# The first seven-product tile's weight forms of the second feed-forward, ordered behind the turned rows of the last block

## The chip, the cores and the metric

The kernel is one program on one core of a Trainium2 chip. It computes a whole decoder layer for 512 tokens. The metric is the device time of one execution in microseconds (us); several runs are taken and the median stands. The engines are TensorE (PE; its weight loads are listed as PEld), VectorE (DVE), ScalarE (ACT), GpSimd (POOL) and SyncE (SP, which here only issues transfers). Each engine works through its own queue of instructions in the order in which they stand in the program, and waits for the others by semaphores.

## The reference

The layer has a first feed-forward, a mixer (dilated attention and a recurrence, gated and merged), and a second feed-forward. Every part has a root-mean-square norm ahead of it and one behind it. The change is at the seam between the mixer's output product and the second feed-forward:

```python
def rms_norm(x, g):
    y = x * lax.rsqrt(jnp.mean(x * x, axis=-1, keepdims=True) + NORM_EPS)
    return y * g

def swiglu(x, w_gate, w_up, w_down):
    return (jax.nn.silu(x @ w_gate) * (x @ w_up)) @ w_down

    ...
    h = h + rms_norm(merged @ w_out[l], mix_norm_post[l])

    f = swiglu(rms_norm(h, ffn2_norm_pre[l]), ffn2_w_gate[l], ffn2_w_up[l], ffn2_w_down[l])
    h = h + 0.5 * rms_norm(f, ffn2_norm_post[l])
```

There are 512 tokens, the model is 1024 wide and the feed-forward 2816, which is 22 tiles of 128 columns. Everything is float32.

## The kernel before

**Products in three.** Each float32 operand is split into a high part (ACT, a copy to a shorter format, line 269) and a low part (DVE, the difference, line 270). A product is three matmuls: high by high, high by low, low by high.

**The seam.** The output product of the mixer works on token rows, in four blocks of 128 tokens. When a block's sums are done, `Boundary.block` works out its scale from the sum of squares (lines 342 to 344 and 383), adds the block to the residual h (DVE, line 475), stores h by a POOL transfer (line 476), squares the new h with a running sum (ACT, line 478), takes the second scale (ACT line 390, DVE lines 342 to 344) and writes the normed rows u in two halves (DVE, line 483). `Boundary.turn` then turns these rows into columns: TensorE transposes (line 491) into a bank, ACT and DVE write the high part (line 494) and the low part (line 495), and ACT copies the bank to `facc` as well (line 496).

**The second feed-forward.** Its first three tiles of 128 columns (0 to 2) are ordinary products of gate and up weights. `gemm_first` runs the first five of the six weights in two halves of 256 tokens (lines 284 to 286): the first half of the tokens, which needs blocks 0 and 1 only, for all five weights, and then the second half. The turns of blocks 2 and 3 are called behind the third and the fourth weight of the first half. So the last block's rows have to be turned before the second half begins. The sixth weight follows in `ffn`.

**Seven-product tiles.** The other 19 tiles (3 to 21) are done by a scheme that needs seven products of half size in place of eight, with forms that are sums of quarters. The forms of x are made in three steps (lines 610 to 616 and splits). For each tile `w_forms_in_place` reads one raw block of up and gate weights of 1 MB and makes four splits (7 forms) from it, with four sums in place (lines 652 to 658). `prod` (from line 1008 on) runs the products in the order p1, p5, p6, p2, p7, p3, p4. In the first such tile ACT copies the bank behind p1 (line 1016), and p6 adds onto the same bank. DVE adds the pieces of the result (line 1021): one of these sums reads the bank behind p7, and p4 adds onto that bank.

**Buffers.** Raw weights have two buffers of 1 MB; SP issues a load (line 215) as soon as a buffer's readers are through. Split weights have four wide slots (`w8`) and two narrow ones (`w4`). The four wide ones are held by the first four ordinary weights while the seam is worked on. Of a seven-product tile's four splits, one is narrow (`d`).

**What sets the order.** The code is traced in program order, and a planner then writes each engine's queue: of the instructions that are ready by its own estimate of the times, the one with the best priority goes next. `high_priority` moves a block of code ahead in priority (the weight forms by 100 steps, the emptying of banks by 200). `tc.issue_after(ins)` adds an order edge: what is traced in its block on the engine of `ins` is put behind `ins` in that engine's queue, without a wait for its end. In `ffn`, `behind(*engines)` uses this with the dictionary `last`, which holds the last instruction of each engine that was named: the forms of a tile are made in `behind("DVE", "ACT")`, so behind the last DVE and ACT instruction of the product before. The dictionary starts empty, so the forms of the first two seven-product tiles, 3 and 4, which are made before any product has run, have no edge.

Of the kernel before, what the change touches and what calls it, by code (L numbers as in the profile page):

```python
# [10 lines left out]
F32 = mybir.dt.float32  # L11
F32R = mybir.dt.float32r
AF = mybir.ActivationFunctionType
# [141 lines left out]
def hybrid_layer(ctx: ExitStack, tc: tile.TileContext, xT: bass.AP, xN: bass.AP, wst: bass.AP,  # L155
                 first: bass.AP, rows: bass.AP, wdn: bass.AP, wbig: bass.AP, consts: bass.AP, bias: bass.AP, out: bass.AP):
    nc = tc.nc
    DVE, ACT, PE = nc.vector, nc.scalar, nc.tensor
# [19 lines left out]
    def new_h():  # L178
        hs["t"] = [bpool.tile([P, 4, T], F32, name="h", tag="b") for _ in range(2)]
# [9 lines left out]
    def fb(b, sl=slice(0, D)):  # L189
        return facc[:, 2 * b:2 * b + 2, :].rearrange("p k t -> p (k t)")[:, sl]  # L190
# [51 lines left out]
    def big(shape, dt=F32R):  # L242
        return bpool.tile(shape, dt, name="big", tag="b")
# [24 lines left out]
    def split(dh, dl, src):  # L268
        ACT.activation(dh, src, AF.Copy)  # L269
        DVE.tensor_sub(dl, src, dh.bitcast(F32))  # L270

    def acc_ps():
        turns["acc"] += 1
        return banks[(turns["acc"] - 1) % turns["n"]]

    def aux_ps():
        turns["aux"] += 1
        return banks[turns["of"][(turns["aux"] - 1) % len(turns["of"])]]
# [26 lines left out]
    def gemm_first(keys, x, slots, then):  # L305


        wts = [fetch(k, None if i < 4 else slots.pop(0)) for i, k in enumerate(keys)]
        pss = [acc_ps() for _ in keys]
        for sl in HALVES:  # L310
            for i, (wt, ps) in enumerate(zip(wts, pss)):
                for k in range(x.n):
                    mm3(ps[:, sl], k128(wt[0])[:, k, :], k128(wt[1])[:, k, :], x.hi[k][:, sl],
                        x.lo[k][:, sl], k == 0, k == x.n - 1)
                if sl.start == 0:
                    for f in then.get(i + 1, ()):
                        f()
        return pss
# [91 lines left out]
    FHALVES = (slice(0, T), slice(T, D))  # L410
# [54 lines left out]
    class Boundary:  # L465
# [21 lines left out]
        def turn(self, b):  # L487
            for i, u in enumerate(self.u.pop(b)):
                ps = aux_ps()
                for j in range(4):  # L490
                    PE.transpose(ps[:, j * P:(j + 1) * P], u[:, j * P:(j + 1) * P], ident)
                src = ps.rearrange("p (k t) -> p k t", k=4)
                hi, lo = (t[:, :, b * P:(b + 1) * P] for t in (self.his[i], self.los[i]))
                ACT.activation(hi, src, AF.Copy)
                DVE.tensor_sub(lo, src, hi.bitcast(F32))
                ACT.activation(fb(b, FHALVES[i]), ps, AF.Copy)

    def act_of(his, los):
        return Act([his[k // 4][:, k % 4, :] for k in range(8)], [los[k // 4][:, k % 4, :] for k in range(8)])
# [54 lines left out]
    def tx_slot(pool, bufs=1):  # L554
        return pool.tile([P, 2, 4, HB], F32R, name="tx", tag="tx", bufs=bufs)

    def forms_of(x, his, los, pool, copied, places={}):


        spool[0] = pool  # L560
        fx = facc.rearrange("p k t -> p (k t)").rearrange("p (b c) -> p b c", b=4)

        def quarter(i, j):
            return fx[:, 2 * j:2 * j + 2, i * T:i * T + T]

        def slot():
            return tx_slot(pool, 1 if copied else 2).rearrange("p s k t -> p s (k t)").rearrange(
                "p s (b c) -> p s b c", b=2)

        x01, x10, x11 = quarter(0, 1), quarter(1, 0), quarter(1, 1)  # L570
        t, d = {}, {}
        for name, i, j in (("p1", 0, 0), ("p2", 1, 0), ("p3", 1, 1)):
            t[name] = tuple(z[i][:, :, HALVES[j]] for z in (his, los))

        def copies():
            for name in ("p1", "p2", "p3"):
                v = big([P, 2, 4, HB])
                for i in range(2):
                    nc.gpsimd.dma_start(v[:, i], t[name][i])
                t[name] = v[:, 0], v[:, 1]  # L580

        def form(name, v, src):
            t[name] = tuple(v[:, i].rearrange("p b (k t) -> p k b t", k=4) for i in range(2))
            split(v[:, 0], v[:, 1], src)

        def first():
            d[1], d[2] = (pool.tile([P, 2, T], F32, name="ts", tag="s", bufs=2) for _ in range(2))
            DVE.tensor_sub(d[1], quarter(0, 0), x01)
            DVE.scalar_tensor_tensor(d[2], x11, -1.0, d[1], op0=ALU.mult, op1=ALU.subtract)
            form("p6", slot(), d[2])  # L590

        def second():
            DVE.tensor_sub(x01, x11, x01)
            form("p7", places["p7"](), x01)

        def third():
            DVE.scalar_tensor_tensor(d[2], d[2], -1.0, x10, op0=ALU.mult, op1=ALU.subtract)
            form("p4", slot(), d[2])

        def fourth():  # L600
            form("p5", places["p5"](), d[1])

        if not copied:
            return t, [first, second, third, fourth]

        def early():
            if copied:
                copies()
            d[1], d[2] = (pool.tile([P, 2, T], F32, name="ts", tag="s", bufs=2) for _ in range(2))
            DVE.tensor_sub(d[1], quarter(0, 0), x01)  # L610
            DVE.scalar_tensor_tensor(d[2], x11, -1.0, d[1], op0=ALU.mult, op1=ALU.subtract)
            DVE.tensor_sub(x01, x11, x01)

        def middle():
            form("p6", slot(), d[2])
            DVE.scalar_tensor_tensor(d[2], d[2], -1.0, x10, op0=ALU.mult, op1=ALU.subtract)
            form("p5", big([P, 2, 2, T]), d[1])

        def late():
            form("p7", big([P, 2, 2, T]), x01)  # L620
            form("p4", big([P, 2, 2, T]) if copied else slot(), d[2])

        return t, [early, middle, late]
# [189 lines left out]
        def rows(self):  # L813
            return self.ub.rearrange("p (s k) t -> p s (k t)", s=2)

    def ffn(n, x, r, forms_x, home, pss):
        t, steps = forms_x
        n0 = NSTD[n]
        ub, wdt, dr = home.ub, home.wd, home.dr
# [50 lines left out]
        def last_act(f):  # L870
            v = home.slot((f - LAST[0] - 1) % 8)
            return v[:, 0, :], v[:, 1, :]
# [108 lines left out]
                    else:  # L981
                        add(u0, True)

        last = {}

        @contextmanager
        def behind(*engines):
# [141 lines left out]
        last = Act(*zip(*(last_act(f) for f in range(*LAST))))  # L1129
# [16 lines left out]
    pss = [acc_ps() for _ in range(4)]  # L1146
# [12 lines left out]


    end1 = ffn(1, u1, r1, x_forms("g1a", r1, ap1), home1, pss)
    new_h()
    for b in range(4):
# [19 lines left out]
    with ExitStack() as mx:  # L1183
# [17 lines left out]
        pss = [acc_ps() for _ in range(4)]  # L1201
# [226 lines left out]
    with ExitStack() as mx:  # L1428
# [130 lines left out]
        for hd in range(NH):  # L1559
# [9 lines left out]
            for kind, c in FILL[hd]:  # L1569
                if kind == "attn":  # L1570
                    ws = fetch((kind, c))
                    for i in range(2):
                        ps = acc_ps()
                        gemm(ps, [w[:, i * T:(i + 1) * T] for w in ws], attn)
                        DVE.tensor_mul(facc[:, 2 * c + i, :], ps, facc[:, 2 * c + i, :])
                else:
                    ps = acc_ps()
# [10 lines left out]
        for c in range(KC):  # L1588
            ps = acc_ps()
# [6 lines left out]
    ap2 = ctx.enter_context(tc.tile_pool(name="act2", bufs=1))  # L1596
    home2 = Home(ap2)
    his, los = ([home2.act[:, 8 * i + 4 * s:8 * i + 4 * s + 4, :] for i in range(2)] for s in range(2))
    u2 = act_of(his, los)
    kept = dpool.tile([4, P, D], F32, name="kept")  # L1600
    grow3, grow4 = gains(home2.rows(), 2, 3)
    bd2 = Boundary(1.0, grow4, his, los, kept)
# [3 lines left out]
    keys = [(w, 2, i) for i in range(NSTD[2]) for w in ("gate", "up")]  # L1606
    pss = gemm_first(keys[:NFIRST], u2, [home2.spare()[2]],
                     {3: [lambda: bd2.turn(2)], 4: [lambda: bd2.turn(3)]})
    end2 = ffn(2, u2, None, forms_of(u2, his, los, ap2, True), home2, pss)
    new_h()  # L1610
    for b in range(4):
        nc.gpsimd.dma_start(hb(b), kept[b])
# [132 lines left out]
```

## Time and profile before

| what | value |
|---|---|
| median of 3 runs | 1223.34 us (1223.24 to 1223.8) |
| the profiled execution's own time | 1223.28 us |
| its span, first to last instruction | 1221.2 us |
| mean granted TensorE clock | 0.999 |
| the seam: first transposes of the last block | 888.66 us into the span |
| first seven-product tile of the second feed-forward: first product | 911.70 us |

A row of the timeline reads: start, duration, engine, line, operation, what is written `<-` what is read, shapes, and in brackets how long the engine stood idle before it and what ended that. When a row has x2 or more, instructions that follow each other are merged. A row of the waits reads: who waited, for whom, total us, number of times, longest. A row of the chain that ended last reads: start, duration, what. A row of stretches reads: the stretch, its length, then busy us and count of TensorE, its weight loads, DVE, ACT and POOL, then the granted clock, the DMA share and GB/s. ACT and DVE instructions overlap a little at their ends, so starts are the better measure of a sequence.

### The profile page before, as it was taken

Reading aid. Unit: us, or ns where it says so; the run is one execution under the profiler, and the core shown is the slowest. Engines: PE = TensorE matmul, PEld = TensorE weight load, DVE = VectorE, ACT = ScalarE, POOL = GpSimd, SP = SyncE. Lnnn points to the kernel's source line nnn. Section 1 sums busy time; section 2 is a strip of 40 time slices with the busy share of each in tenths; the row PEclk is TensorE's granted clock in tenths of the full one; section 3 lists DMA queues with packets and bytes.
Section 4 is the critical chain, followed back from the end, with each engine's and each line's share of the span. In section 5 each row is a group of like instructions: output and inputs, shape, how many; then the busy total and the mean of one; then the engine's idle time right before and its main releaser. Section 6 shows DMA issues by size and latency. Waiting matters only on the chain.

```text
span 1221.2 us, 19573 instructions
## 1 busy us (share of the span) xinstructions
PE 1209.9 (99%) x7790; PEld 1102.6 (90%) x7790; DVE 984.0 (81%) x1540; ACT 746.0 (61%) x1238; POOL 84.5 (7%) x139
## 2 busy tenths in 40 slices
PE   9999999999999999999999999999999999999998
PEld 8898989999878899999999888888899999999996
DVE  7998878988579888888776998755789887979864
ACT  6566665655656564666666788634566665656452
POOL 0001111100102000000001000000110110101000
PEclk9999999999999999999999999999999999999999
DMA  6336646464735222223235223524462655555441
GB/s 247 138 104 173 170 111 171 141 163 121 255 116 176 105 82 101 78 79 104 70 138 202 75 91 141 183 101 164 132 190 87 182 155 146 159 136 163 114 156 69
DMA packets 37452, 167.63 MB, mean 137 GB/s; under 512 B 4209, under 2 KB 7665, under 8 KB 25329
## 3 DMA queue, kind: packets, MB, share of 16 engines
q1 hardware_dynamic: 18432, 107.13, 25.2%
q0 software_dynamic: 18928, 59.25, 18.1%
q8 instruction: 61, 1.00, 0.3%
q14 instruction: 31, 0.25, 0.1%
HBM read 153.79 MB, written 8.39 MB: 133 GB/s over the span
## 4 chain that ended last, share of the span: by engine, by line
PE 93%; DVE 4%; issue 1%; DMA 1%; ACT 1%; DVEq 0%; ACTq 0%
PE bank L1008 10%; PE bank L1009 9%; PE bank L1010 9%; PE bank L284 7%; PE bank L286 7%; PE bank L285 7%; PE bank L675 6%; PE bank L676 6%; PE bank L677 6%; PE bank L923 4%; PE bank L922 4%; PE bank L924 4%; PE bank L405 3%; PE bank L406 3%; PE bank L404 3%; DVE w L270 1%
## 5 line engine op out<-in xcount | busy, mean ns | idle before, releaser
L270 DVE TENSOR_TENSOR w<-raw,w 128x1024 fp32r<-128x1024 f32 (+1 forms) x276 | 300.6, 1100 | 61.9 <-ACT w L269 56.0
L269 ACT ACTIVATE w<-raw 128x1024 fp32r<-128x1024 f32 (+1 forms) x276 | 258.9, 956 | 102.4 <-PE bank L286 40.1
L1008 PE MATMUL bank<-big,w 128*128 128x256 f32 x840 | 240.6, 286 | 2.5 <-ACT c L1016 0.9
L1009 PE MATMUL bank<-big,w 128*128 128x256 f32 x840 | 237.5, 283 | 0.0
L1010 PE MATMUL bank<-big,w 128*128 128x256 f32 x840 | 236.2, 283 | 0.0
L1008 PEld LDWEIGHTS bank<-big,w 128*128 128x128 f32 x840 | 160.8, 191 | 7.3 <-ACT c L1016 1.9
L1009 PEld LDWEIGHTS bank<-big,w 128*128 128x128 f32 x840 | 160.9, 192 | 1.6
L1010 PEld LDWEIGHTS bank<-big,w 128*128 128x128 f32 x840 | 160.3, 192 | 0.0
L922 PE MATMUL bank<-wd,act 128*128 128x512 f32 x224 | 87.8, 392 | 0.0
L923 PE MATMUL bank<-wd,act 128*128 128x512 f32 x224 | 87.8, 392 | 0.0
L924 PE MATMUL bank<-wd,act 128*128 128x512 f32 x224 | 87.2, 389 | 0.0
L675 PE MATMUL bank<-big,w 128*128 128x256 f32 x252 | 73.0, 290 | 0.0
L677 PE MATMUL bank<-big,w 128*128 128x256 f32 x252 | 71.5, 284 | 0.0
L676 PE MATMUL bank<-big,w 128*128 128x256 f32 x252 | 71.2, 283 | 0.0
L1016 ACT ACTIVATE c<-bank 128x256 f32<-128x256 f32 x72 | 27.5, 382 | 61.3 <-PE bank L1010 60.8
L270 DVE TENSOR_TENSOR wd<-npair,wd 128x1024 fp32r<-128x1024 f32 x24 | 29.4, 1224 | 37.7 <-ACT wd L269 37.7
L284 PE MATMUL bank<-act,w 128*128 128x512 f32 (+1 forms) x168 | 58.6, 354 | 0.0
L285 PE MATMUL bank<-act,w 128*128 128x512 f32 (+1 forms) x168 | 58.5, 349 | 0.0
L286 PE MATMUL bank<-act,w 128*128 128x512 f32 (+1 forms) x168 | 58.5, 349 | 0.0
L284 PE MATMUL bank<-big,w 128*128 128x512 f32 x144 | 56.0, 389 | 0.0
L285 PE MATMUL bank<-big,w 128*128 128x512 f32 x144 | 56.0, 389 | 0.0
L286 PE MATMUL bank<-big,w 128*128 128x512 f32 x144 | 56.0, 389 | 0.0
(399 smaller groups left out, 3208.7 us busy)
## 6 DMA issues: line engine op xcount, KB each, us to landing
raw<-in_w SPq DMA_DIRECT2D x90, 1024.0 KB, 4.9
dr<-in_wdn POOLq DMA_DIRECT2D x40, 512.0 KB, 5.8
npair<-in_wdn POOLq DMA_DIRECT2D x32, 512.0 KB, 5.5
big<-act POOLq DMA_DIRECT2D x6, 512.0 KB, 4.1
h<-in_x SPq DMA_DIRECT2D x8, 256.0 KB, 5.2
h<-in_xn POOLq DMA_DIRECT2D x4, 512.0 KB, 5.2
raw<-in_wbig SPq DMA_DIRECT2D x2, 1024.0 KB, 4.8
kept_m<-h POOLq DMA_DIRECT2D x4, 512.0 KB, 2.9
```

Source lines behind the costliest of these rows:

```text
L269: ACT.activation(dh, src, AF.Copy)
L270: DVE.tensor_sub(dl, src, dh.bitcast(F32))
L284: PE.matmul(ps, wh, xh, start=first, stop=False)
L285: PE.matmul(ps, wh, xl, start=False, stop=False)
L286: PE.matmul(ps, wl, xh, start=False, stop=last)
L675: PE.matmul(ps, wh, xh, start=start and k == 0, stop=False, skip_group_check=True)
L676: PE.matmul(ps, wh, xl, start=False, stop=False, skip_group_check=True)
L677: PE.matmul(ps, wl, xh, start=False, stop=k == 3, skip_group_check=True)
L922: PE.matmul(ps, xh, wh, start=start and k == 0, stop=False, skip_group_check=True)
L1008: PE.matmul(ps, wh, xh, start=start and k == 0, stop=False, skip_group_check=True)
L1009: PE.matmul(ps, wh, xl, start=False, stop=False, skip_group_check=True)
L1010: i = PE.matmul(ps, wl, xh, start=False, stop=k == 3, skip_group_check=True)
```

## The change

The turn keeps the last DVE and the last ACT instruction that it wrote, and the second feed-forward's dictionary `last` starts with these two in place of empty. The first feed-forward still starts with an empty one. So the weight forms of tile 3, and those of tile 4, stand behind the last turned rows of the last block in the queues of DVE and ACT.

```diff
@@ Boundary.turn
                 ACT.activation(hi, src, AF.Copy)
-                DVE.tensor_sub(lo, src, hi.bitcast(F32))
-                ACT.activation(fb(b, FHALVES[i]), ps, AF.Copy)
+                i_dve = DVE.tensor_sub(lo, src, hi.bitcast(F32))
+                i_act = ACT.activation(fb(b, FHALVES[i]), ps, AF.Copy)
+            self.last = {"DVE": i_dve.ins, "ACT": i_act.ins}
@@ ffn
-    def ffn(n, x, r, forms_x, home, pss):
+    def ffn(n, x, r, forms_x, home, pss, after={}):
...
-        last = {}
+        last = dict(after)
@@ the call
-    end2 = ffn(2, u2, None, forms_of(u2, his, los, ap2, True), home2, pss)
+    end2 = ffn(2, u2, None, forms_of(u2, his, los, ap2, True), home2, pss, bd2.last)
```

The dictionary is used where the forms are made:

```python
            elif ev[0] == "prep":
                with behind("DVE", "ACT"):
                    forms[ev[1]] = w_forms_in_place(("gu", n, ev[1]))
```

## The prediction

> **What bounds the kernel now.** I read the page's busy times first, then the waits of TensorE, then the chain that ended last around the place of the change, then the three queues' timelines there.
>
> ```profile
> span 1221.2 us, 19573 instructions
> PE 1209.9 (99%) x7790; PEld 1102.6 (90%) x7790; DVE 984.0 (81%) x1540; ACT 746.0 (61%) x1238; POOL 84.5 (7%) x139
> ...
> PE bank L491 <- DVE u L483: 1.4, 1, 1.4
> ```
>
> TensorE is busy for 1209.9 of 1221.2 us, so the kernel is bound by TensorE, and a change that adds or removes no matmul can win only what TensorE idles. The longest single wait is that of the transposes of the last boundary block (L491) for the DVE instruction that makes their rows (L483). It stands at this place of the TensorE queue:
>
> ```profile
> 886.97 0.28 PE L286 MATMUL bank<-act,tx 128*128 128x256 f32 x1
> 888.66 0.63 PE L491 MATMUL bank<-cst,u 128*128 128x128 f32 x4 [1.42 <-DVE u L483]
> ```
>
> The gap is 1.42 us: 886.97 + 0.28 = 887.25 to 888.66. The chain that ended last says what made the rows late:
>
> ```profile
> 876.95 6.54 DMA raw<-in_w
> 883.52 0.64 ACT w L269
> 884.18 0.70 DVE w L270
> 884.91 0.70 DVE raw L654
> 885.63 0.69 DVE raw L655
> 886.40 0.60 DVE act L495
> 887.07 0.60 DVE act L495
> 887.77 0.76 DVE u L483
> ```
>
> The raw weights of seven-product tile 3 land at 883.49; one split of them (ACT L269, DVE L270) and two sums (L654, L655) follow, and only behind these the work on the last block. That this work had been ready earlier is seen on ACT and DVE:
>
> ```profile
> 880.86 1.28 DVE L475 SCALAR_TENSOR_TENSOR h<-facc,stat,h 128x1024 f32<-128x1024 f32 x1
> ...
> 883.52 0.63 ACT L269 ACTIVATE w<-raw 128x512 fp32r<-128x512 f32 x1 [4.18 <-DMA raw<-in_w]
> 884.05 1.04 ACT L478 ACTIVATE facc<-h 128x1024 f32<-128x1024 f32 x1
> ...
> 885.57 0.28 ACT L390 ACTIVATE stat<-stat,eps 128x1 f32<-128x1 f32 x1
> ...
> 884.18 0.69 DVE L270 TENSOR_TENSOR w<-raw,w 128x512 fp32r<-128x512 f32 x1 [2.04 <-ACT w L269]
> ...
> 886.25 0.15 DVE L342 SCALAR_TENSOR_TENSOR stat<-stat 128x1 f32<-128x1 f32 x1
> ```
>
> The square of the last block (L478) had its rows at 880.86 + 1.28 = 882.14, but ACT stood 4.18 us in front of the weight split, waiting for the load, and the square came at 884.05, 1.91 us later. DVE stood 2.04 us in the same way.
>
> **The change, part by part.** The two names kept in turn and the copied dictionary issue nothing. They add order edges from the last DVE and ACT instruction of the last block's turn to every DVE and ACT instruction of the weight forms of tiles 3 and 4; an edge within one queue is no wait and costs nothing by itself. Of these forms all but four instructions already stand behind the turn (the first other one, tile 3's next split, is on ACT at 898.73), so what moves is one ACT instruction of 0.63 us (883.52) and three DVE instructions (884.18, 884.91, 885.63; from 884.18 to the next one at 886.25 they take 2.07 us). No DMA moves: the raw load is outside the edges, on SP, and waits only for its buffer. POOL gets nothing new; its copies of the turned forms wait for the turn and can only come sooner.
>
> Step 1, the stall. With the split gone from ahead of it, L478 starts at 882.14. From its start to the end of L390 it took 884.05 to 885.85, so 1.80; L390 ends at 883.97. From the first DVE step (886.25) to the end of the first half of the rows (887.77 + 0.76 = 888.53) it took 2.28, with two turned forms of the block before it in between, to which nothing is added: the first half is there at about 886.3, the second some 0.7 later, and TensorE asks at 887.25. The stall goes with 0.3 to 1 us to spare: -1.42 us, and TensorE is that much earlier from here.
>
> Step 2, where the moved work lands. These are rows of DVE, ACT, SP and TensorE between the turn and the first seven-product tile:
>
> ```profile
> 889.96 1.35 DVE L495 TENSOR_TENSOR act<-bank,act 128x512 fp32r<-128x512 f32 x2 [0.78 <-ACT act L494]
> 891.32 1.22 DVE L610 TENSOR_TENSOR ts<-facc 128x1024 f32<-128x1024 f32 x1
> 892.65 1.23 DVE L611 SCALAR_TENSOR_TENSOR ts<-facc,ts 128x1024 f32<-128x1024 f32 x1
> ...
> 894.93 1.22 DVE L270 TENSOR_TENSOR big<-ts,big 128x1024 fp32r<-128x1024 f32 x1
> 896.06 1.22 DVE L270 TENSOR_TENSOR w<-raw,w 128x1024 fp32r<-128x1024 f32 x1
> ...
> 890.68 1.26 ACT L496 ACTIVATE facc<-bank 128x512 f32<-128x512 f32 x2
> ...
> 898.73 1.04 ACT L269 ACTIVATE w<-raw 128x1024 fp32r<-128x1024 f32 x1
> ...
> 903.19 0.63 ACT L269 ACTIVATE w<-raw 128x512 fp32r<-128x512 f32 x1 [0.98 <-DMA raw<-in_w]
> ...
> 911.12 1.06 ACT L269 ACTIVATE big<-ts 128x1024 fp32r<-128x1024 f32 x1 [2.62 <-DVE ts L616]
> 912.08 0.61 ACT L269 ACTIVATE act<-ub 128x512 fp32r<-128x512 f32 x1
> 912.60 1.04 ACT L269 ACTIVATE w<-raw 128x1024 fp32r<-128x1024 f32 x1
> 913.55 0.36 ACT L1016 ACTIVATE c<-bank 128x256 f32<-128x256 f32 x1
> ...
> 897.31 0.33 SPq L215 DMA_DIRECT2D raw<-in_w  x1
> ...
> 911.70 0.28 PE L1008 MATMUL bank<-big,w 128*128 128x256 f32 x1
> ...
> 914.57 0.28 PE L1008 MATMUL bank<-tx,w 128*128 128x256 f32 x1
> ```
>
> On ACT the moved split follows the two copies L496, which end at 890.68 + 1.26 = 891.94, or 890.53 with step 1. It ends at 891.16. On DVE the turn then ends at 889.9, L610 fits before the split's other half is ready, and the three moved instructions run from 891.16 to 893.23. The rest of the queue, from L611 on, comes at 893.23 instead of 892.65: 0.58 us later on the clock, 2.0 later against TensorE. The forms themselves have time: tile 3's first product starts at 911.70, and its first weights were split from 898.73 on.
>
> Step 3, what is late next. The wait that takes over is that of the third product of tile 3 (914.57, it adds onto the bank of the first) for ACT's copy of that bank (L1016), which ended at 913.55 + 0.36 = 913.91. So it had 0.66 us to spare. The product wants to start 1.42 earlier, the copy is ready to run as soon as the first product ends, but on ACT three splits stand ahead of it (911.12, 912.08, 912.60), and the first of these waited 2.62 us for DVE's L616. If DVE's and ACT's queues keep their times on the clock there, 1.42 - 0.66 = 0.76 us is given back, and -0.66 is left. Both ends: if the queue moves along with TensorE nothing is given back (-1.42). If it keeps its old order and the 0.58 of step 2, all but 0.08 goes back: the split of the last ordinary weight (896.06) frees the raw buffer for the load at 897.31, whose landing gates ACT at 903.19 and then DVE up to L616, so 0.58 passes down the chain. If that split is put ahead of the split of form p5 that stands before it (894.93, 1.22), the load starts 0.58 - 1.22 = 0.64 earlier than before instead. I take the middle, -0.66, since it lies between an order that passes on +0.58 and one that passes on -0.64, and the trace cannot say which the planner writes.
>
> That ACT keeps this order, even with the copy ready, is seen in L478's 1.91 us above. The Trainium skill (TensorE: Matmul & The Clock Gate, on the architecture of the array, engine queue depths) says that ACT and DVE are strict first-in first-out queues; by that rule the copy cannot pass the splits, and the sum would be -0.66 with the order on the clock, against -1.42 if an engine took what is ready. The trace agrees at L478.
>
> Sum: -1.42 + 0.76 = -0.66. The profiled execution took 1223.28 us (span 1221.2 and 2.08 around it), 0.06 under the median 1223.34; so about 1222.7 in either measure.
>
> **The rivals.**
>
> *Whole gain kept* (1221.9): the copy L1016 is planned ahead of the splits, or DVE's queue is refilled tightly. For it: DVE idles between the turn and tile 3. Against it: the next wait is on the clock of a load and two queues.
>
> *Whole gain given back, or not taken*: the 0.58 of step 2 goes through, or other work takes the place of the split ahead of L478, so that the rows stay late. -1.42 + 1.34 = -0.08, so 1223.3. For it: no instruction is removed, DVE has the same 2.07 us to do later. Against it: nothing else of the queues was found waiting for a load at 882.14.
>
> *Slower*: DVE becomes the bound in the first seven-product tiles. In the 20 us after 920 it has no room:
>
> ```profile
> 920.00:940.00 20.00, 20.00 (x168) 19.86 (x167) 19.64 (x32) 14.63 (x26) 0.00 (x0) 1.00 0.30 106
> ...
> 919.95 0.42 DVE L1021 TENSOR_TENSOR ub<-bank,c 128x256 f32<-128x256 f32 x1
> ...
> 920.42 0.38 PE L1008 MATMUL bank<-big,w 128*128 128x256 f32 x1
> ```
>
> DVE is busy 19.64 of 20 us (third busy column). Tile 3's last product (920.42) starts right behind the sum that must read its bank first (919.95 + 0.42 = 920.37), without any reserve, so each us by which that sum is later costs a us. If the moved work pushes one more split of 1.22 us (as at 896.06) ahead of this sum in tiles 3, 4 and 5, that is 3.66 - 1.42 = +2.24, so 1225.6. It decides from 1.42 us of such delay on. Against it: the sums are given priority in the plan. It is the only mechanism here that ends well above the old time.
>
> **How the numbers follow.** About 0.2% (2.4 us) is what a measurement of this kernel can tell from no change. Part of the gain kept (-0.2 to -1.2): 0.42, with 1222.1 to 1223.1 as its own range. Whole gain (1221.9 and a little below): 0.20. Nothing left (within 0.2 us): 0.15. Slower by the full queue: 0.23, half of it past 0.2%. Even the whole stall is 0.12%, so "faster by over 0.2%" needs other waits to go as well: 0.04; slower by over 0.2%: 0.12; within: 0.84. The range goes from a little below the whole gain, 1221.6, to a little short of the slower case's price, 1225.2, which leaves about 0.05 below it and 0.13 above.
>
> **What would show it.** After: no wait of L491 for L483; L478 on ACT right behind the block's L475; the weight split and L654, L655 behind the last L495 and L496. Step 3 is right if TensorE has a new wait of some tenths at L1008 for ACT L1016 or DVE L1021 around 913 to 920, and wrong if there is none and the span is 1.4 shorter. The prediction fails if a wait of over 1.5 us appears in the first tiles of the second feed-forward, or a different order brings waits further down.

## The result, and the profile after

The changed kernel takes 1222.05 us (median of 22 runs), against 1223.27 us for the kernel before in the same comparison: a ratio of 0.9988 with a 95% interval of 0.9983 to 0.9994, so 0.7 to 2.1 us less. The forecast was 1222.7, which is 0.6 us under; about 1.2 us were won, nearly twice that. The profiled execution took 1222.07 us.

The page and the waits of TensorE in the changed kernel (lines behind 495 have moved by one, so L1009 is the former L1008, L1017 the former L1016, L1022 the former L1021):

```profile
span 1220.2 us, 19574 instructions
PE 1210.3 (99%) x7790; PEld 1102.9 (90%) x7790; DVE 983.5 (81%) x1540; ACT 746.0 (61%) x1238; POOL 84.3 (7%) x139
...
PE bank L1145 <- DVE eps L201: 1.1, 1, 1.1
PE bank L1009 <- ACT c L1017: 0.9, 2, 0.5
PE bank L1009 <- DVE u L1022: 0.9, 1, 0.9
```

The wait of L491 for L483 is gone from the list, and no other has come into it: the wait at the start and those of 0.9 us lie in the first feed-forward or before it. Here is ACT's queue at the seam after the change, then DVE's, then TensorE's:

```profile
882.48 1.06 ACT L478 ACTIVATE facc<-h 128x1024 f32<-128x1024 f32 x1 [2.83 <-DVE h L475]
...
884.08 0.28 ACT L390 ACTIVATE stat<-stat,eps 128x1 f32<-128x1 f32 x1
...
888.79 1.27 ACT L496 ACTIVATE facc<-bank 128x512 f32<-128x512 f32 x2
889.96 0.62 ACT L269 ACTIVATE w<-raw 128x512 fp32r<-128x512 f32 x1
```

```profile
885.88 1.41 DVE L483 SCALAR_TENSOR_TENSOR u<-h,stat,ub 128x512 f32<-128x512 f32 x2
888.07 1.36 DVE L495 TENSOR_TENSOR act<-bank,act 128x512 fp32r<-128x512 f32 x2 [0.78 <-ACT act L494]
889.42 1.22 DVE L611 TENSOR_TENSOR ts<-facc 128x1024 f32<-128x1024 f32 x1
890.61 0.69 DVE L270 TENSOR_TENSOR w<-raw,w 128x512 fp32r<-128x512 f32 x1
891.22 1.22 DVE L612 SCALAR_TENSOR_TENSOR ts<-facc,ts 128x1024 f32<-128x1024 f32 x1
892.36 0.68 DVE L655 TENSOR_TENSOR raw<-raw 128x512 f32<-128x512 f32 x1
892.96 1.22 DVE L613 TENSOR_TENSOR facc<-facc 128x1024 f32<-128x1024 f32 x1
894.09 0.69 DVE L656 TENSOR_TENSOR raw<-raw 128x512 f32<-128x512 f32 x1
894.70 1.22 DVE L270 TENSOR_TENSOR big<-ts,big 128x1024 fp32r<-128x1024 f32 x1
```

```profile
886.77 1.29 PE L491 MATMUL bank<-cst,u 128*128 128x128 f32 x8
```

The square L478 waits only for its own rows, and the moved split and the two sums (L655, L656) stand behind the turn, one by one between the first forms of x. The transposes have moved too: they now stand ahead of the fifth weight's first matmuls, where before six of these came first.

The two profiled executions do not agree to the last tenth. At the seam's last common instruction before the change bites, the square of the third block, the changed kernel is 0.32 us *later* (875.39 before, 875.71 after; a difference of this kind is there from the first feed-forward on, where the code is the same). Tile 3's first product starts at 910.65 in place of 911.70. So the seam itself is 1.05 + 0.32 = 1.37 us shorter, close to the 1.42 us of the wait. From tile 3 on the two run in parallel to within 0.06 us for all of the second feed-forward's 19 tiles.

Around tile 3, where the forecast had expected the next wait:

```profile
903.08 1.58 ACT L269 ACTIVATE w<-raw 128x512 fp32r<-128x512 f32 x2 [1.91 <-DMA raw<-in_w]
905.39 1.06 ACT L269 ACTIVATE tx<-ts 128x1024 fp32r<-128x1024 f32 x1 [0.72 <-PE bank L286]
...
910.15 1.06 ACT L269 ACTIVATE big<-ts 128x1024 fp32r<-128x1024 f32 x1 [2.70 <-DVE ts L617]
...
912.59 0.36 ACT L1017 ACTIVATE c<-bank 128x256 f32<-128x256 f32 x1
```

```profile
910.65 0.28 PE L1009 MATMUL bank<-big,w 128*128 128x256 f32 x1
...
913.52 0.28 PE L1009 MATMUL bank<-tx,w 128*128 128x256 f32 x1
```

The copy of the first bank ends at 912.59 + 0.36 = 912.95, and p6 starts at 913.52: the reserve is 0.57 us, against 0.66 before. The copy did not stay on the clock. It came 0.96 us sooner, or 1.28 with the 0.32 us taken off, where TensorE came 1.37 sooner. What released it is the chain that the forecast named: ACT's narrow split of tile 4's weights waits for its load, DVE's half follows and then DVE's queue up to L617 (the former L616), and the first of the three splits ahead of the copy (910.15) waits for that. DVE's rows, after and then before:

```profile
901.96 0.68 DVE L659 TENSOR_TENSOR raw<-raw 128x512 f32<-128x512 f32 x1
902.58 0.69 DVE L836 TENSOR_TENSOR ub<-bank,g 128x512 f32<-128x512 f32 x1
903.74 0.69 DVE L270 TENSOR_TENSOR w<-raw,w 128x512 fp32r<-128x512 f32 x1 [0.48 <-ACT w L269]
...
908.90 1.21 DVE L617 SCALAR_TENSOR_TENSOR ts<-ts,facc 128x1024 f32<-128x1024 f32 x1
```

```profile
903.86 0.69 DVE L270 TENSOR_TENSOR w<-raw,w 128x512 fp32r<-128x512 f32 x1 [0.77 <-ACT w L269]
904.47 0.68 DVE L658 TENSOR_TENSOR raw<-raw 128x512 f32<-128x512 f32 x1
...
905.67 0.68 DVE L835 TENSOR_TENSOR ub<-bank,g 128x512 f32<-128x512 f32 x1
...
909.87 1.22 DVE L616 SCALAR_TENSOR_TENSOR ts<-ts,facc 128x1024 f32<-128x1024 f32 x1
```

Two things brought the copy forward. The narrow split on ACT got its weights a little sooner: 903.08 in place of 903.19, so 0.43 us with the offset taken off. And from this split to the one at 910.15 it is 7.07 us in place of 7.93 (903.19 to 911.12): a weight sum (L659, the former L658) and an elementwise product of an ordinary tile (L836, the former L835) now stand ahead of the split that waits for the load, where before they stood behind it. Together that is 0.43 + 0.86 = 1.29 us.

### The profile page after: what moved, and what is told of

It reads as the page before. It is cut to its first block, busy times and chain, and to the rows that moved or that the text cites. A ratio compares the mean times of both kernels' runs of the same rounds, so it can differ in the third digit from the quotient of the medians.

```text
span 1220.2 us, 19574 instructions
## 1 busy us (share of the span) xinstructions
PE 1210.3 (99%) x7790; PEld 1102.9 (90%) x7790; DVE 983.5 (81%) x1540; ACT 746.0 (61%) x1238; POOL 84.3 (7%) x139
## 4 chain that ended last, share of the span: by engine, by line
PE 97%; DVE 1%; ACT 1%; issue 0%; DVEq 0%; ACTq 0%
PE bank L1009 10%; PE bank L1010 9%; PE bank L1011 9%; PE bank L284 7%; PE bank L286 7%; PE bank L285 7%; PE bank L676 6%; PE bank L677 6%; PE bank L678 6%; PE bank L924 4%; PE bank L923 4%; PE bank L925 4%; PE bank L404 3%; PE bank L406 3%; PE bank L405 3%; PE bank L750 1%
## 5 line engine op out<-in xcount | busy, mean ns | idle before, releaser
L270 DVE TENSOR_TENSOR w<-raw,w 128x1024 fp32r<-128x1024 f32 (+1 forms) x276 | 300.1, 1097 | 61.0 <-ACT w L269 55.2
L1009 PE MATMUL bank<-big,w 128*128 128x256 f32 x840 | 240.6, 286 | 2.5 <-ACT c L1017 0.9
L1009 PEld LDWEIGHTS bank<-big,w 128*128 128x128 f32 x840 | 160.8, 191 | 7.3 <-ACT c L1017 1.9
L1017 ACT ACTIVATE c<-bank 128x256 f32<-128x256 f32 x72 | 27.6, 383 | 61.2 <-PE bank L1011 60.8
L270 DVE TENSOR_TENSOR wd<-npair,wd 128x1024 fp32r<-128x1024 f32 x24 | 29.3, 1222 | 37.7 <-ACT wd L269 37.7
```

The costliest lines, as they stand in the source:

```text
L1009: PE.matmul(ps, wh, xh, start=start and k == 0, stop=False, skip_group_check=True)
```

## The experiments

Totals are medians, each beside runs of the kernel before on the same chip. No kernel leaves work out; what differs is the order of instructions, or how often one is done.

**ACT's edge or DVE's?** Theory: ACT, standing in front of a load, made the rows late. Rival: the 2.07 us of form work on DVE. A version with the ACT edge alone was not run. In the code DVE's three instructions follow on ACT's split (the low part needs the high part, the first sum overwrites what both read, and the second what the first reads), so an ACT edge would hold them back too. This version has the DVE edge alone:

```diff
-    end2 = ffn(..., home2, pss, bd2.last)
+    end2 = ffn(..., home2, pss, {"DVE": bd2.last["DVE"]})
```

> The changed kernel with the DVE edge alone. On ACT the narrow weight split of tile 3 is again ahead of the square of the last block (L478) and waits for its load; on DVE the split and the two sums stay behind the turn. Theory A (ACT standing in front of the load is the main cause of the wait): L478 again at 884 us, the rows' first half ready about 887.1, the second about 887.8, and TensorE, whose transposes now stand right behind the fourth weight (886.4), waits 0.9 to 1.2 us; so only 0.2 to 0.5 us of the gain is left against the kernel before. Theory B (the 2.07 us of form work on DVE is the main cause): the wait of L491 is under 0.4 us and the gain is 1.0 us or more.

Measured: 1223.82 us against 1223.72, ratio 0.9999 (0.9990 to 1.0007). All of the gain is gone. In the trace, from the third block's square to tile 3's first product, it is 912.29 - 876.10 = 36.19 us, against 36.31 in the kernel before and 34.94 in the changed one. ACT and TensorE at the seam with the DVE edge alone:

```profile
884.15 0.63 ACT L269 ACTIVATE w<-raw 128x512 fp32r<-128x512 f32 x1 [4.11 <-DMA raw<-in_w]
884.69 1.04 ACT L478 ACTIVATE facc<-h 128x1024 f32<-128x1024 f32 x1
```

```profile
888.90 0.63 PE L491 MATMUL bank<-cst,u 128*128 128x128 f32 x4 [1.30 <-DVE u L483]
```

DVE had none of the forms in its way, and TensorE still waited 1.30 us. The cause is ACT's queue: it stood idle for 4.11 us in front of one small split whose load had not come. Theory A holds, and more strongly than I gave it: I had expected 0.2 to 0.5 us of the gain to stay; 0.12 stayed in the trace and nothing in the total. I had taken the transposes to stand right behind the fourth weight, as in the changed kernel; here the planner put three of the fifth weight's matmuls ahead of them.

**How far back must the forms go?** Here they are tied only behind the last block's square on ACT and its rows on DVE:

```diff
+            i_y = ACT.activation(fb(b), hb(b), AF.Square, accum_out=t)
...
+                i_u = DVE.scalar_tensor_tensor(u, hb(b, fs), r, self.grow[:, fs], ...)
+            self.rows_made = {"DVE": i_u.ins, "ACT": i_y.ins}
...
-    end2 = ffn(..., home2, pss, bd2.last)
+    end2 = ffn(..., home2, pss, bd2.rows_made)
```

> The changed kernel with the forms tied behind the last block's square on ACT (L478) and its rows on DVE (L483), and no longer behind the whole turn. Theory A (what has to stand ahead of the load is the square and what follows it up to the rows, so the narrow split must not be ahead of the second scale on ACT, L390): ACT stands in front of the load between L478 and L390, the rows come 0.3 to 0.5 us later than in the changed kernel, L491 waits 0.2 to 0.5 us, total 0.9 to 1.2 us under the kernel before. Theory B (the square alone matters): no wait, total as in the changed kernel.

Measured: 1222.03 us against 1223.44, ratio 0.9988 (0.9979 to 0.9997), and no wait of L491. ACT's queue in this kernel:

```profile
882.16 1.06 ACT L478 ACTIVATE facc<-h 128x1024 f32<-128x1024 f32 x1 [2.84 <-DVE h L475]
883.13 0.18 ACT L478 ACTIVATION_READ_ACCUMULATOR facc<-h 128x1 f32 x1
883.39 0.63 ACT L269 ACTIVATE w<-raw 128x512 fp32r<-128x512 f32 x1
883.93 0.28 ACT L390 ACTIVATE stat<-stat,eps 128x1 f32<-128x1 f32 x1
```

My theory A for this run fell. The split now stands between the square and the second scale, but it starts 0.08 us after the square is through (883.31), so it costs its 0.6 us and nothing for the load. One place further back in ACT's queue was enough for the whole gain. That hangs on when the load lands: in the kernel before it landed at 883.49, so the margin here is next to none.

**Did the gain hang on the earlier transposes?** The planner had put the transposes six matmuls (0.72 us) earlier, which I had not foreseen. If step 3 had been right for the place that it assumed, it should show here:

```diff
                 for k in range(x.n):
+                    if sl.start == 0 and i == 4 and k == 2:
+                        bd2.turn(3)        # in place of behind the fourth weight
                     mm3(...)
```

> The changed kernel with the last block's transposes called behind the first six matmuls of the fifth weight, where they stood in the kernel before (in the changed kernel the planner put them ahead of these six). Theory A (the queues behind the seam have room; the early transposes were not needed for the gain): the turned rows come 0.72 us later, the wait of L491 stays away, p6 of tile 3 does not wait, total 1.2 to 1.6 us under the kernel before. Theory B (step 3 as predicted holds once the turn is where it was assumed to be): TensorE waits 0.5 to 0.8 us for ACT's copy of the first bank or for DVE's sums in tile 3, total 0.5 to 0.9 under.

Measured: 1221.72 us against 1223.44, ratio 0.9986 (0.9977 to 0.9995), with no wait of L491 and none at p6. Tile 3's first products and the copy in this kernel:

```profile
909.83 0.28 PE L1012 MATMUL bank<-big,w 128*128 128x256 f32 x1
...
912.70 0.28 PE L1012 MATMUL bank<-tx,w 128*128 128x256 f32 x1
```

```profile
911.46 0.38 ACT L1020 ACTIVATE c<-bank 128x256 f32<-128x256 f32 x1
```

The copy has 912.70 - 911.84 = 0.86 us of reserve here, more than before. With the turn where it was assumed to be, the planner put the last ordinary weight's split ahead of the p5 form on DVE (the earlier of the two orders that the forecast weighed), and the next load left 14.41 us ahead of tile 3's first product (at 895.42) in place of 13.57 in the changed kernel (at 897.08). Theory A holds for this order. The other of the two orders, with the turn at this place and the load later, was not run.

**The sum that stood behind a load.** In the kernel before, the last sum of tile 3's forms stood on DVE behind tile 4's split, which waits for a load. The changed kernel has it ahead. This version puts it back:

```diff
+            # key ("gu", 2, 4): an order edge from its narrow DVE split to tile 3's g1 sum
+            tc.add_manual_dep(g1_sum_of_tile_3, narrow_low_of_tile_4.name, NoSync)
```

> The changed kernel with one more order edge on DVE: the last sum of tile 3's weight forms (g1) stands behind tile 4's narrow split, which waits for a load, as it stood in the kernel before. Theory A (the chain p6 split, p4 split, copy of the first bank starts from TensorE's release of the p6 slot and was free of the load only because this sum was planned ahead): the p6 split on ACT starts 0.6 to 0.8 us later than in the changed kernel, the copy behind p1 too, its reserve of 0.57 us is gone and p6 waits 0.1 to 0.3 us; total 1.0 to 1.3 us under the kernel before. Theory B (step 3 as predicted): p6 waits about 0.76 us and the total is 0.66 under. Theory C (the place of this sum does not matter): copy and total as in the changed kernel, no wait.

Measured: 1221.87 us against 1223.72, ratio 0.9985 (0.9976 to 0.9994); no wait at p6. ACT's rows (this execution is 2.57 us later at the seam, by its second L496 at 891.36):

```profile
907.70 1.06 ACT L269 ACTIVATE w<-raw 128x1024 fp32r<-128x1024 f32 x1 [1.42 <-DVE raw L665]
908.66 1.04 ACT L269 ACTIVATE tx<-ts 128x1024 fp32r<-128x1024 f32 x1
...
915.41 0.36 ACT L1023 ACTIVATE c<-bank 128x256 f32<-128x256 f32 x1
```

The p6 split is 908.66 - 2.57 - 905.39 = 0.70 us later, as theory A said, but the copy only 915.41 - 2.57 - 912.59 = 0.25. The copy does not hang on the p6 split but on DVE's L617, and there the sum's 0.60 us filled a gap of 0.35 us (by starts) that DVE has in the changed kernel behind the narrow split: L617 starts 0.25 later. So the first half of theory A was right and its end was not; theory C has the total. The place of this one sum is not why the gain was kept. The elementwise product L836 stayed ahead of the waiting split in this kernel, and a version with both behind it and the rest as in the changed kernel was not run. An estimate from these rows: the copy would come 0.25 + 0.60 = 0.85 us later against a reserve of 0.57, and some 0.3 us would be given back.

**Twice the moved work.** Tile 3's narrow DVE split is done four times:

```diff
             split(d[:, 0, :], d[:, 1, :], u1)
+            for _ in range(3 if key == ("gu", 2, 3) else 0):
+                DVE.tensor_sub(d[:, 1, :], u1, d[:, 0, :].bitcast(F32))
```

> The changed kernel with the DVE half of tile 3's narrow split done four times in place of once (the same values), so about 1.8 us of DVE work more behind the turn: twice the work that the change moved. Theory A (up to tile 3's first products the DVE queue stands idle often enough to take in the moved work, and as much again): no wait over 0.2 us in tile 3, total within 0.3 us of the changed kernel. Theory B (DVE's time passes through to ACT's copy of the first bank, with 0.57 us of reserve): a wait of 0.7 to 1.2 us in tile 3, total 0.2 to 0.7 us under the kernel before.

Measured: 1221.86 us against 1223.44, ratio 0.9986 (0.9977 to 0.9995): the changed kernel's gain, whole. No wait in tile 3. The queues between the turn and tile 3 took in 1.8 us more of DVE work, with the planner setting other things back for it: the weight sum and the elementwise product stand behind the waiting split again, but a split of 0.6 us that had stood ahead of L617 now stands behind it, and from the narrow split on ACT to the one behind L617 it is 910.03 - 902.71 = 7.32 us. Theory A holds, with a queue that the planner wrote anew.

**The copy's reserve, used up.** ACT's copy of the first bank is done four times:

```diff
-            c1 = copy(b) if lead else None
+            c1 = copy(b, 4 if n == 2 else 1) if lead else None    # the copy in a loop
```

> The changed kernel with ACT's copy of the first bank in tile 3 of the second feed-forward done four times in place of once (the same values; three more ACT instructions of some 0.3 us). Theory A (the reserve in front of p6 is the 0.57 us seen in the trace, and what goes beyond it is paid in full): ACT is 0.9 to 1.0 us longer there and TensorE waits 0.3 to 0.5 us at p6, total 0.8 to 1.1 us under the kernel before. Theory B (TensorE has other work to put there, or the time is made good later): no wait, total 1.2 to 1.4 under.

Measured: 1222.16 us against 1223.72, ratio 0.9989 (0.9980 to 0.9997). TensorE in tile 3:

```profile
910.33 0.28 PE L1009 MATMUL bank<-big,w 128*128 128x256 f32 x1
...
913.64 0.39 PE L1009 MATMUL bank<-tx,w 128*128 128x256 f32 x1
```

From p1 to p6 it is 3.31 us in place of 2.87. Of these 0.44 us the planner used 0.24 for two matmuls of p2 that it put ahead; about 0.2 us is lost, and the total can't tell it from none. The limit that step 3 named is real: p6 does wait once the copy is late. The copy just was not late.

**The slower rival's price.** The sum that p4 of tile 3 waits for is done four times:

```diff
-            sum_of(u[:, hi_], b, c5)
+            for _ in range(4 if n == 2 and f == 3 else 1):
+                sum_of(u[:, hi_], b, c5)
```

> The changed kernel with the DVE sum that p4 of tile 3 waits for (second feed-forward) done four times in place of once (the same values); the planner also lets one split and one other sum in between, so the last of the four ends about 2.2 us later than the one sum did. Theory A (the slower rival's price: no reserve in front of p4): TensorE waits about 2 us there, all of it stays in the total, which is 0.5 to 1 us over the kernel before. Theory B (a reserve of over 1 us, or the time is made good): wait under 1 us, total not above the kernel before.

Measured: 1225.74 us against 1223.44, ratio 1.0017 (1.0009 to 1.0026). TensorE's waits, then its rows behind p3 of tile 3, then DVE's sums there:

```profile
PE bank L1009 <- DVE u L1022: 1.9, 1, 1.9
PE bank L1009 <- DVE g L1022: 1.8, 1, 1.8
```

```profile
922.24 0.36 PE L1009 MATMUL bank<-big,w 128*128 128x256 f32 x1 [1.82 <-DVE g L1022]
...
923.26 0.28 PE L1009 MATMUL bank<-big,w 128*128 128x256 f32 x1
```

```profile
921.68 0.41 DVE L1022 TENSOR_TENSOR g<-bank,c 128x256 f32<-128x256 f32 x1
922.01 0.88 DVE L1022 TENSOR_TENSOR ub<-bank,c 128x256 f32<-128x256 f32 x2
```

The row at 922.24 is not p4 yet: the last two of the four sums, which p4 waits for, end at 922.89. By the order and number of the matmuls it is the start of tile 4's p5, eight matmuls that the planner put ahead; p5 waits for the sum g, and this stands on DVE behind the second of the four sums. p4 follows at 923.26. So DVE's lateness became a wait of 1.82 us, and by p6 of tile 4 TensorE is 1.99 us behind the changed kernel (15.13 us from tile 3's first product in place of 13.14). The kernel ended slower than before. That rival's mechanism is right; it was not set off, since in the changed kernel the same sum came 1.05 us earlier, with TensorE. The total is higher than this one wait explains, and the first row shows why in part: the wait in the first feed-forward, 0.9 us in the changed kernel's profile, is 1.9 here. The rest, about half a us, is open. What makes that wait long or short is the next experiment's matter.

**The same edge elsewhere.** The 0.9 us wait of the first feed-forward looks alike: in tile 8 DVE does the p6 and p7 down forms (L270) ahead of the sum that p4 waits for. This version ties the p7 form behind that sum:

```diff
-                for a, p in due:
-                    down_form(a, p)
+                for a, p in due[:len(due) - len(held_back)]:    # held_back = due[1:] for n == 1, f == 8
+                    down_form(a, p)
             product("p7", b, False)
             sum_of(u[:, hi_], b, c5)
+            with behind("copy", "sum"):                         # last["sum"] is kept in sum_of
+                for a, p in held_back:
+                    down_form(a, p)
```

> The changed kernel with a second edge of the same kind, in the first feed-forward: in tile 8 the DVE half of the p7 down form stands behind the sum that p4 waits for (in the changed kernel TensorE waits 0.91 us there). Theory A (a wait caused by a form standing ahead on DVE goes when the form is put behind, and TensorE keeps the gain because everything behind is released by TensorE): the 0.91 us wait falls to under 0.15, total 1.9 to 2.2 us under the kernel before. Theory B (the gain is given back at the next tile): the wait goes but the total is as in the changed kernel, 1.2 to 1.4 under.

Measured: 1221.17 us against 1223.72, ratio 0.9980 (0.9972 to 0.9989), so 2.55 us less, more than either theory gave. To see whether the two gains add up, each edge alone and both (the same kernel once more) were then timed side by side on one chip:

> The kernel before with the edge of the first feed-forward alone (tile 8's p7 down form on DVE behind the sum that p4 waits for), without the change at the seam. Theory A (the two waits are independent and each is worth what TensorE waits in it): the wait at the sum falls from 0.9 or more to under 0.2, L491 still waits 1.4; total 0.7 to 1.5 us under the kernel before (the wait was 0.9 us in three profiles and 1.5 to 1.9 in three others). Theory B (they share one reserve): under 0.4.

> The changed kernel itself, beside the other two on the same chip. Total 1.1 to 1.5 us under the kernel before.

> Both edges, beside each alone on the same chip. Theory A (independent): the sum of the two gains, 2.0 to 2.9 us under the kernel before. Theory B (one reserve): no more than the larger of the two.

| kernel | median, us | ratio to before (1223.27) | less than before, us |
|---|---|---|---|
| p7 edge alone | 1222.65 | 0.9994 (0.9985 to 1.0003) | 0.62 |
| the change alone | 1221.85 | 0.9988 (0.9979 to 0.9996) | 1.42 |
| both edges | 1221.34 | 0.9984 (0.9976 to 0.9993) | 1.93 |

The medians add up (0.62 + 1.42 = 2.04 against 1.93), as theory A has it. But the p7 edge alone is not clear of no change and came 0.08 us under its range, both together came 0.07 under theirs, and the intervals of the change alone and of both edges overlap, so these totals do not exclude theory B. Waits of TensorE with both edges:

```profile
PE bank L1009 <- ACT bank L1030: 0.2, 1, 0.2
PE bank L1009 <- DVE u L1022: 0.2, 1, 0.2
```

The wait at the sum falls from 0.9 to 0.2 us. Both edges together are the fastest kernel of this study by the medians. The wait that they take away is also one that varies from execution to execution: it was 0.9 us in most of the profiles and 1.5 to 1.9 in those of three kernels, though their first feed-forward is the same. In each of the three long ones ACT waits 0.43 to 0.90 us for a load from GpSimd's queue ahead of the p6 form; this is the row of the kernel with the sum behind the load:

```profile
108.93 1.06 ACT L269 ACTIVATE wd<-npair 128x1024 fp32r<-128x1024 f32 x1 [0.90 <-DMA npair<-in_wdn]
```

## Why the prediction was right, and where it was not

**The way and the range.** Faster by less than 0.2%, by the wait named, was right, and the measured 1222.05 us lies in the stated range, near its lower end. The size was short: -0.66 was said, and -1.2 came (-1.37 in the trace at the seam). The rival *whole gain kept* (1221.9) is what happened, and by the second of the two ways that it gave: DVE's queue was refilled more tightly.

**Step 1** held to a tenth of a us once the 0.32 us between the executions is taken off: L478 at 882.16 (said 882.14), the end of L390 at 884.04 (said 883.97; 882.14 + 1.80 is 883.94), the first half of the rows at 885.88 + 0.76 - 0.32 = 886.32 (886.3). The cause is now shown, not only argued: with the DVE edge alone the wait is back.

**Step 2** said that DVE's queue behind the turn would be 0.58 us later on the clock. It was earlier: the p5 form starts at 894.70 in place of 894.93, so 0.23 sooner, and 0.55 with the offset taken off. Two terms were mis-sized. The turn ended 1.88 us earlier (889.43 against 891.31; 2.20 corrected) where 1.41 was assumed, mostly since the planner put the transposes ahead of six matmuls that had stood before them; that is 0.79 us. And the moved work cost 1.65 us, not 2.07: placed one by one between independent instructions, each of the three took 0.60 to 0.61 from start to start, where in the old chain they took 0.62 to 0.73; the rest came from a gap behind the first form of x (L611, the former L610) that was filled.

**Step 3** is the step that failed: "If DVE's and ACT's queues keep their times on the clock there, 1.42 - 0.66 = 0.76 us is given back." Its path was right, from a load over ACT and DVE's queue up to L616 to the splits and the copy, but the times on it were not kept. The forecast took the middle between a load 0.58 us later on the clock and one 0.64 sooner, so about nothing. It was issued 0.23 us sooner (897.08 against 897.31), 0.55 with the offset taken off, and the split that it releases came 0.43 sooner, corrected. Behind it the path was 0.86 us shorter, because the planner had put two DVE instructions ahead of the split that waits. So the reserve in front of p6 went from 0.66 to 0.57 us, and nothing was given back.

It is not that the queues follow TensorE here. Some splits on ACT are released by TensorE (905.39 above), but these were not what the copy waited for last. The kernel with the copy done four times has the changed kernel's queues up to there, and shows what it waits for:

```profile
902.30 1.58 ACT L269 ACTIVATE w<-raw 128x512 fp32r<-128x512 f32 x2 [1.46 <-DMA raw<-in_w]
...
909.37 1.06 ACT L269 ACTIVATE big<-ts 128x1024 fp32r<-128x1024 f32 x1 [2.25 <-DVE ts L617]
```

From the split that the load releases to the split behind L617 it is 7.07 us, as in the changed kernel, and it is 7.07 or 7.08 in all six profiles with this order. The first of the two lies between 26.91 and 27.37 us behind the third block's square in these six, as the load lands; tile 3's first product lies 34.92 to 34.94 us behind it in all of them. So the path moves with the load and not with TensorE. That the new order took 0.86 us out of it was the planner's doing, and I had not foreseen it; without it, by the estimate given with the sum behind the load, some 0.3 us would have gone back. What the experiments add is that the planner found such an order each time: with 1.8 us more of DVE work, with the sum put back, and with the turn later, there was no new wait.

**The first-in first-out rule.** The Trainium skill (TensorE: Matmul & The Clock Gate, on the architecture of the array, engine queue depths) says that ACT and DVE are strict first-in first-out queues. The traces agree: with the DVE edge alone, L478 again stood behind a split that waited 4.11 us, and came at 884.69 though its rows were there at 882.85. But -0.66 does not follow from the rule, which says nothing on when what stands ahead is released. That was my inference, and it failed.

**The other rivals.** *Given back or not taken*: no other work took the split's place on ACT; L478 waited for its own rows alone. *Slower*: the price is real (1.82 us of wait when the sum is done four times), the condition did not come up.

## What to carry to other kernels

When a wait of the bounding engine is removed, follow the work ahead of each next wait back to what released it last. What hangs on a load moves with the load, and can take the gain back when the bounding engine comes earlier; here that path was 7.07 us long wherever the load landed. An instruction that waits for a load should not stand ahead of ready work in the same queue, even if it is short: on ACT it cost 1.4 us here through a split of 0.6 us, and moving it a single place back was enough, since the load had landed by then. On DVE two instructions of 0.6 us each, moved ahead of such a split, took 0.86 us out of the path. And where a planner writes the queues, a new edge reorders neighbours as well, so a forecast should say which of them could move.

## What was not expected of the hardware

DVE instructions of 128x512 that do not use each other's result follow at 0.60 us from start to start, though each lasts 0.68 to 0.69; where one works on the result of the one ahead (L654, L655 in the kernel before: 884.91 and 885.63), it is 0.72. Mixing two dependent chains in one queue thus saved about 0.1 us per instruction.

The same code in the first feed-forward lost 0.9 us in some executions and 1.9 in others. In the long ones a load's landing is seen to hold ACT; what moves the landing is left open.
